# Hybrid decoder block on one core: order and halves of the first loads and casts, a warm-up on another operand, and other buffers for the down projection's weight chunks

## The chip, the cores and the metric

The kernel runs on one core of a Trainium2 chip. The metric is device time of one execution in microseconds (us); lower is better. Where several runs were made, the median is given. Engines are named as the profile names them: PE does matrix products (PEld is its loading of weights), DVE is the vector engine, ACT the scalar engine, POOL is GpSimd, SP only issues transfers. A name with a q behind it (SPq, ACTq, POOLq) is an engine's instruction stream issuing a DMA.

## The reference, cut to what matters

The input is x of 512 rows and 1024 columns in float32. All weights are float32.

```python
h = rmsnorm(x, pre_mix_norm)
q_r, k_r, v_r, g_r, q_s, k_s, v_s, gate_r, gate_s = split(h @ w_in)
y_r = (silu(g_r) * groupnorm(retention(q_r, k_r, v_r))) @ w_ret_out
y_s = sliding_window_attention(q_s, k_s, v_s, sinks) @ w_swa_out
x = x + rmsnorm((sigmoid(gate_r) * y_r + sigmoid(gate_s) * y_s) @ w_out, post_mix_norm)
h = rmsnorm(x, pre_mlp_norm)
u = square(relu(h @ w_up))
x = x + rmsnorm(u @ w_down, post_mlp_norm)
```

The change touches the very first product (k_s and v_s, together 256 columns of w_in) and the last one (u @ w_down, where w_down has 4096 rows and 1024 columns).

## The kernel before, in words

**Two-part operands.** A float32 factor is cut into a high part and a low part: `split` (L156) lets ACT cast the source to the rounded type fp32r (the high part, L158), and DVE subtract that from the source (the low part, L160). `split_scaled` (L400) does the same for a source times the pre-norm gain gT (ACT L402, DVE L403). `mm3` (L215) makes each product from three matmuls: high by high (L218), high by low (L219), low by high (L220). Its second argument is the moving operand: for k_s and v_s that is the weights `wkv`, and `xg` is loaded as the stationary one. So the first L218 needs the high parts of xg and wkv, the first L219 needs the low part of wkv, the first L220 the low part of xg.

**The start.** x comes transposed in eight blocks of 128 x 512, `xTs[:, k]`, and the weights of k_s and v_s in eight pieces of 128 x 256, `raw_kv[:, k]`. SP issues them in turn; the piece for k = 0 is issued by ACT, behind the gain. Until the first operands are there, ten products of the identity with itself (WARM, L397) keep PE at work. Then the loop at L409 does two splits and twelve matmuls for each k, into four PSUM banks `ptok`. Two query blocks (tile `pblk`, split from `raw_q`) follow, then the matmuls that spread the row factors (L451), two more query blocks, and from then on blocks that read the normalized input `hT`, which DVE and ACT make from `xTs` in `norm_input` (L427). Next come the `wide` products of v_r, and between them the window attention: scores into `swa_s` (L506), a softmax on DVE (L520 to L538) and ACT (L527), and transposes of the probabilities `s` on PE (L550, L552), first for one head of a pair and then for the other.

**The end.** The up projection runs in sixteen pairs, `up_pair` (L1274). The three that matter here are the last steps of the last pair: `last["chain"]`, `last["chain2"]` and `last["chain3"]` are the ACT copies of its sums. The down projection is a Strassen-Winograd scheme over 2 x 2 blocks: the steps at L1373 (`step_p1`, `step_p2`, `step_p5` for four chunks j each), then `step_p6`, `step_p3`, `step_p7` (L1421 to L1446) and p4. A step splits a chunk of u (`left`, L1313, 128 x 1024 at a time) and a chunk of w_down (`right`, L1318, two halves of 128 x 1024), and then makes 24 matmuls of 128 x 512 (`product2`). The chunks of w_down, 1 MB each, come in two kinds. `tch[j]` stays for several steps and has other chunks added to it by transfers that POOL issues (`t_add`, L1333). `load_b` (L1336) brings chunks that are used once or twice.

**Buffers and order.** `raw_tile` (L162) hands out two buffers in turn, which the whole kernel shares; a transfer into one waits until the split of its last content is done. `dpool3` (L1301) uses space that the up projection frees, so a transfer into it waits for the last products that read from there. Each engine does its instructions in the order in which they are queued. That order is made before the run, from priorities (`tc.high_priority`) and from explicit edges: `tc.issue_after(ins)` queues what a block contains behind `ins` on that engine.

Of the kernel before, what the change touches and what calls it, by code (L numbers as in the profile page):

```python
# [10 lines left out]
F32 = mybir.dt.float32  # L11
# [5 lines left out]
P = 128  # L17
D_MODEL = 1024
# [13 lines left out]
CHAIN_AHEAD = 400  # L32
SUMS_AHEAD = 0
HSUM_AHEAD = 400
WARM = 10
LEFT_AHEAD = 300
T2_DMA = 4
ENTRY = 32
# [2 lines left out]
C_QR, C_KR, C_VR, C_GR, C_QS, C_KS, C_GATE_R = (0, 512, 1024, 2048, 3072, 3584, 3840)  # L41
# [63 lines left out]
def f(ap):  # L105
    return ap.bitcast(F32)
# [3 lines left out]
def block_kernel(ctx, tc, x, xT, pre_mix, w_in, w_qk, w_v, w_g, w_gate, w_ret, w_swa, w_out, sinks, post_mix,  # L110
                 pre_mlp, w_up, w_down, post_mlp, decay, chunk, dist, out):
    nc = tc.nc
    x, out = x[0], out[0]
    w_in, w_ret, w_swa, w_out = (w[0] for w in (w_in, w_ret, w_swa, w_out))
# [6 lines left out]
    def bank(shape, name="ps"):  # L121
        return psum.tile(shape, F32, tag="ps", name=name)
# [5 lines left out]
    ident = const.tile([P, P], F32, name="ident")  # L128
# [25 lines left out]
    last = {}  # L154

    def split(hi, lo, src):  # L156

        last["hi"] = nc.scalar.copy(hi, src)  # L158
        last["prior"] = last.get("split")
        last["split"] = nc.vector.tensor_tensor(lo, src, f(hi), op=ALU.subtract)  # L160

    def raw_tile(shape):  # L162
        return stream.tile(shape, F32, name="raw", tag="raw", bufs=2)

    def place(shape, front=False):

        whole = stream.tile([P, 1024 + 64], F32R, name="whi", tag="whi")
        flat = whole[:, :1024] if front else whole[:, 16 : 16 + 1024]
        dims = " ".join("abc"[: len(shape) - 1])
        sizes = {n: shape[i + 1] for i, n in enumerate("abc"[: len(shape) - 1])}  # L170
        hi = flat.rearrange(f"p ({dims}) -> p {dims}", **sizes)
        if "wlo" not in last:
            pad(stream, 64)
            last["wlo"] = True
        return hi, stream.tile(shape, F32R, name="wlo", tag="wlo")

    def parts(src, shape, front=False):
        hi, lo = place(shape, front)
        split(hi, lo, src)
        return hi, lo  # L180
# [34 lines left out]
    def mm3(ps, a, b, first, last, more=False):  # L215

        (ah, al), (bh, bl) = a, b
        nc.tensor.matmul(ps, ah, bh, start=first, stop=False, skip_group_check=more)  # L218
        nc.tensor.matmul(ps, ah, bl, start=False, stop=False, skip_group_check=more)  # L219
        return nc.tensor.matmul(ps, al, bh, start=False, stop=last, skip_group_check=more)  # L220
# [147 lines left out]
    xTs = xTpool.tile([P, KD, SEQ], F32, name="xTs", tag="xs")  # L368
    xgctx = ExitStack()
    xgpool = xgctx.enter_context(tc.tile_pool(name="xgpool", bufs=1, side="right"))  # L370
    gT = xgpool.tile([P, KD], F32, name="gT")
    xg = [xgpool.tile([P, KD, SEQ], F32R, name=f"xg{i}") for i in range(2)]
    xctx = ExitStack()
    xpool = xctx.enter_context(tc.tile_pool(name="xpool", bufs=1))
    ones = xpool.tile([P, P], F32, name="ones")
    wkv = [xpool.tile([P, KD, 256], F32R, name=f"wkv{i}") for i in range(2)]

    nc.vector.memset(ones, 1.0)
    raw_kv = raw_tile([P, KD, 256])
    for k in range(KD):  # L380
        nc.sync.dma_start(xTs[:, k], xT[k])
        if k == 0:
            nc.scalar.dma_start(gT, pre_mix)
        queue = nc.scalar if k == 0 else nc.sync
        queue.dma_start(raw_kv[:, k], w_in[k * P : (k + 1) * P, C_KS : C_KS + 256])
    raw_q = raw_tile([P, KD, 256])
    for i in range(2):
        rows = slice(i * D_MODEL // 2, (i + 1) * D_MODEL // 2)
# [6 lines left out]
        nc.sync.dma_start(xts[t], x[t * P : (t + 1) * P, :])  # L395
    warm = bank([P, P], "warm")
    for _ in range(WARM):  # L397
        nc.tensor.matmul(warm, ident, ident, start=True, stop=True)

    def split_scaled(hi, lo, src, scale):  # L400

        nc.scalar.mul(hi, src, scale)  # L402
        nc.vector.scalar_tensor_tensor(lo, src, scale, f(hi), op0=ALU.mult, op1=ALU.subtract)  # L403

    def xcol(k, t):
        return tuple(a[:, k, t * P : (t + 1) * P] for a in xg)

    kv_ps = [bank([P, 256], "ptok") for _ in range(NT)]
    for k in range(KD):  # L409
        split(wkv[0][:, k], wkv[1][:, k], raw_kv[:, k])  # L410
        split_scaled(xg[0][:, k], xg[1][:, k], xTs[:, k], gT[:, k : k + 1])
        for t in range(NT):
            mm3(kv_ps[t], xcol(k, t), tuple(a[:, k] for a in wkv), k == 0, k == KD - 1)

# [675 lines left out]
    for bp in range(KD // 2):  # L1090
# [3 lines left out]
        for b in range(2):  # L1094
            hi = mpool.tile([P, SEQ], F32R, name="mhi", tag="m")
# [30 lines left out]
    for half in range(2):  # L1126
# [11 lines left out]
        with tc.high_priority(offset=CHAIN_AHEAD):  # L1138
            for t in range(2):
# [4 lines left out]
                for n in range(2):  # L1144
                    c = slice(n * 512, (n + 1) * 512)
# [110 lines left out]
    dpool2 = ctx.enter_context(tc.tile_pool(name="dpool2", bufs=1, side="right"))  # L1256
    uc[2] = dpool2.tile([P, 4, 4, 256], F32, name="uc2")
    tch = [None] * 4

    def load_t(j):  # L1260
        pool = dpool2 if j == 0 else dpool3
        tch[j] = pool.tile([P, 4, 512], F32, name=f"tch{j}")
        nc.sync.dma_start(tch[j], w_down[0, 0, j])

    usum = []
# [8 lines left out]
    def up_pair(fp, a):  # L1274
# [19 lines left out]
        return a  # L1294

    load_t(0)
    a = wino_first(up_weights(NH))
    for fp in range(NH, 16):
        a = up_pair(fp, a)
    uctx.close()  # L1300
    dpool3 = ctx.enter_context(tc.tile_pool(name="dpool3", bufs=1))  # L1301
    for j in range(1, 4):
        load_t(j)
    g_out = dpool3.tile([P, D_MODEL], F32, name="g_out")
    nc.sync.dma_start(g_out, post_mlp.to_broadcast([P, D_MODEL]))
    p1c = [dpool3.tile([P, 512], F32, name="p1c", bufs=2) for _ in range(2)]
    p15 = [dpool3.tile([P, 512], F32, name="p15", bufs=2) for _ in range(2)]
    u3 = [dpool3.tile([P, 512], F32, name="u3", bufs=2) for _ in range(2)]
# [4 lines left out]
    def left(j, q):  # L1313
        hi, lo = (ring.tile([P, 4, 256], F32R, name=f"left{i}") for i in range(2))
        split(hi, lo, uc[j][:, q])
        return hi, lo

    def right(src):  # L1318
        return [parts(src[:, 2 * i : 2 * i + 2], [P, 2, 512]) for i in range(2)]
# [8 lines left out]
    def product2(ps, j, a, b):  # L1328
        for h in range(2):
            for tb in range(2):  # L1330
                product(ps, a, b, h, j == 0, j == 3, tb)

    def t_add(dst, k, c, j):  # L1333
        nc.gpsimd.dma_start(dst, w_down[k, c, j], accum_op=ALU.add)

    def load_b(k, c, j, alone=2):  # L1336
        raw = stream2.tile([P, 4, 512], F32, name="rb") if j == alone else raw_tile([P, 4, 512])
        nc.sync.dma_start(raw, w_down[k, c, j])
        return raw

    stream2 = ctx.enter_context(tc.tile_pool(name="stream2", bufs=1))
# [7 lines left out]

    def step_p1(j):  # L1350
        with tc.high_priority(offset=LEFT_AHEAD if j == 0 else 0):
            with tc.issue_after(last["chain"].ins):
                a = left(j, 0)
            with tc.issue_after(last["chain2"].ins):
                b = right(tch[j])
        t_add(tch[j], 0, 1, j)
        product2(p1, j, a, b)

    def step_p2(j):
        with tc.issue_after(last["chain2"].ins), tc.high_priority(offset=LEFT_AHEAD if j == 0 else 0):  # L1360
            a, b = left(j, 2), right(load_b(1, 0, j, 4))
        product2(p2, j, a, b)
# [10 lines left out]
    for step, j in ((step_p1, 0), (step_p2, 0), (step_p1, 1), (step_p5, 0), (step_p2, 1),  # L1373
                    (step_p1, 2), (step_p5, 1), (step_p2, 2), (step_p1, 3), (step_p5, 2),
                    (step_p2, 3), (step_p5, 3)):
        step(j)

    outz = [None] * NT
    ms0 = [None] * NT
# [39 lines left out]
    rb = {}  # L1419
# [18 lines left out]
    for j in range(4):  # L1438
        rb[j] = load_b(1, 1, j)
        step_p6(j)  # L1440
        step_p3(j)
        if j == 0:
            p7 = banks2("p7")
        else:
            step_p7(j - 1)
# [16 lines left out]
    for j in range(2):  # L1462
        a, b = left(j, 3), right(tch[j])
# [21 lines left out]
    for i in range(2):  # L1485
        c = slice(i * 256, (i + 1) * 256)
# [54 lines left out]
```

## Time and profile before

| | us |
|---|---|
| median of 3 runs | 715.14 |
| the three runs | 715.14, 717.18, 713.86 |
| the profiled execution | 716.0 |
| span of its instructions | 714.2 |

The span is counted from the first profiled instruction to the last, and 1.8 us of the profiled execution's own time lie around it. All positions below are microseconds from the span's start. In a row of the timeline the first number is the start, the second the duration, and a bracket at the end gives how long the engine was idle before it and what ended the idle time. "x20" is a count. In a table of windows each engine has its busy time and, in brackets, its count of instructions; DMA share is the mean busy share of the 16 DMA engines.

| engine | busy us | share of the span |
|---|---|---|
| PE | 705.6 | 99% |
| PEld | 631.6 | 88% |
| DVE | 535.0 | 75% |
| ACT | 431.4 | 60% |
| POOL | 63.0 | 9% |

### The profile page before, as it was taken

To read this page: it belongs to the slowest core of one execution; us is meant where nothing else is said; L and a number is where in the kernel's file an instruction comes from. 1 tells how busy PE (TensorE), PEld (TensorE's weight loads), DVE (VectorE), ACT (ScalarE), POOL (GpSimd) and SP (SyncE) were. 2 spreads that over 40 slices of the span, in tenths; PEclk is the share of its full clock that TensorE was granted. 3 is DMA by queue.
4 is the path that set the end of the run, shared out by engine and by line. 5 is a ranking of instruction groups with operands and counts; after the bars stand their busy time and mean duration, and the time that the engine had idled before them with its cause. 6 is when DMAs were issued, how large, how long until landed. Compare 5 with 4: busy or idle time off the path is not lost.

```text
span 714.2 us, 11458 instructions
## 1 busy us (share of the span) xinstructions
PE 705.6 (99%) x4528; PEld 631.6 (88%) x4528; DVE 535.0 (75%) x800; ACT 431.4 (60%) x733; POOL 63.0 (9%) x78
## 2 busy tenths in 40 slices
PE   9999999999999999999999999999999999999996
PEld 8887789898888999989888999999999888888885
DVE  6598978685975667566945876777777787977797
ACT  6657876566655625435733866766668656555571
POOL 0210000121100000000011100000000000010010
PEclk9999999999999999999999999999999999999998
DMA  9964723866444455553662619776753999698603
GB/s 319 331 173 84 163 60 125 244 155 140 90 145 121 126 141 149 155 169 98 217 257 78 162 45 284 199 195 174 197 150 119 329 270 237 145 208 195 117 1 117
DMA packets 40613, 119.37 MB, mean 167 GB/s; under 512 B 3568, under 2 KB 17008, under 8 KB 34416
## 3 DMA queue, kind: packets, MB, share of 16 engines
q1 hardware_dynamic: 33504, 81.28, 32.6%
q0 software_dynamic: 6768, 37.23, 28.0%
q8 instruction: 35, 0.57, 0.3%
q10 hardware_dynamic: 288, 0.14, 0.1%
q14 instruction: 18, 0.15, 0.1%
HBM read 116.54 MB, written 2.10 MB: 166 GB/s over the span
## 4 chain that ended last, share of the span: by engine, by line
PE 91%; DVE 4%; DMA 2%; issue 1%; ACT 1%; POOL 0%; POOLq 0%; DVEq 0%; SPq 0%; ACTq 0%
PE wino L218 9%; PE wino L219 9%; PE wino L220 9%; PE p L220 5%; PE p L219 5%; PE p L218 5%; PE wide L218 4%; PE wide L219 4%; PE wide L220 4%; PE pblk L220 2%; PE pblk L219 2%; PE pblk L218 2%; PE yr L220 2%; PE yr L218 2%; PE ps L218 2%; PE ps L220 2%
## 5 line engine op out<-in xcount | busy, mean ns | idle before, releaser
L160 DVE TENSOR_TENSOR wlo<-raw,whi 128x1024 fp32r<-128x1024 f32 (+1 forms) x80 | 96.3, 1208 | 43.7 <-ACT whi L158 43.6
L158 ACT CAST whi<-raw 128x1024 fp32r<-128x1024 f32 (+1 forms) x80 | 82.8, 1041 | 31.4 <-DMA raw<-in_w_down 7.7
L220 PE MATMUL p<-whi,left 128*128 128x512 f32 x216 | 84.1, 390 | 0.2 <-DVE left L160 0.2
L219 PE MATMUL p<-wlo,left 128*128 128x512 f32 x216 | 84.2, 390 | 0.0
L218 PE MATMUL p<-whi,left 128*128 128x512 f32 x216 | 84.0, 390 | 0.1
L220 PEld LDWEIGHTS p<-whi,left 128*128 128x128 f32 x216 | 40.5, 188 | 9.4 <-DVE left L160 1.1
L219 PEld LDWEIGHTS p<-wlo,left 128*128 128x128 f32 x216 | 40.5, 188 | 8.8 <-DVE wlo L160 0.3
L218 PEld LDWEIGHTS p<-whi,left 128*128 128x128 f32 x216 | 40.5, 188 | 8.7 <-ACT left L158 0.5
L158 ACT CAST p<-rs 128x1024 fp32r<-128x1024 f32 x22 | 23.1, 1052 | 36.5 <-DVE rs L272 36.4
L160 DVE TENSOR_TENSOR wlo<-tch,whi 128x1024 fp32r<-128x1024 f32 x32 | 38.6, 1219 | 7.5 <-ACT whi L158 7.5
L158 ACT CAST left<-uc 128x1024 fp32r<-128x1024 f32 x28 | 29.3, 1051 | 22.8 <-PE p L219 20.9
L160 DVE TENSOR_TENSOR left<-uc,left 128x1024 fp32r<-128x1024 f32 x28 | 34.1, 1220 | 9.9 <-ACT left L158 9.9
L158 ACT CAST whi<-tch 128x1024 fp32r<-128x1024 f32 x32 | 33.2, 1050 | 11.8 <-PE p L220 6.5
L160 DVE TENSOR_TENSOR p<-rs,p 128x1024 fp32r<-128x1024 f32 x22 | 27.0, 1225 | 16.7 <-ACT p L158 16.7
L160 DVE TENSOR_TENSOR wlo<-rs,whi 128x1024 fp32r<-128x1024 f32 x23 | 28.1, 1223 | 12.9 <-ACT whi L158 10.3
L218 PE MATMUL wino<-h2s,p 128*128 128x256 f32 x104 | 28.7, 276 | 0.0
L219 PE MATMUL wino<-h2s,p 128*128 128x256 f32 x104 | 28.7, 276 | 0.0
L220 PE MATMUL wino<-h2s,p 128*128 128x256 f32 x104 | 28.7, 276 | 0.0
L218 PE MATMUL wino<-h2c,whi 128*128 128x256 f32 x104 | 28.7, 276 | 0.0
L219 PE MATMUL wino<-h2c,whi 128*128 128x256 f32 x104 | 28.7, 276 | 0.0
L220 PE MATMUL wino<-h2c,wlo 128*128 128x256 f32 x104 | 28.7, 276 | 0.0
L218 PE MATMUL wino<-h2s,whi 128*128 128x256 f32 x104 | 28.7, 276 | 0.0
(410 smaller groups left out, 2352.1 us busy)
## 6 DMA issues: line engine op xcount, KB each, us to landing
tch<-in_w_down POOLq DMA_DIRECT2D x12, 1024.0 KB, 9.9
raw<-in_w_down SPq DMA_DIRECT2D x7, 1024.0 KB, 7.6
rs<-in_w_up SPq DMA_DIRECT2D x13, 512.0 KB, 4.5
rs<-in_w_up POOLq DMA_DIRECT2D x13, 512.0 KB, 5.5
raw<-in_w_up SPq DMA_DIRECT2D x13, 512.0 KB, 5.3
acc<-in_w_v POOLq DMA_DIRECT2D x4, 1024.0 KB, 8.0
rs<-in_w_gate SPq DMA_DIRECT2D x8, 512.0 KB, 3.8
acc<-in_w_g POOLq DMA_DIRECT2D x4, 1024.0 KB, 8.0
```

The lines of the kernel that those rows point to most:

```text
L158: last["hi"] = nc.scalar.copy(hi, src)
L160: last["split"] = nc.vector.tensor_tensor(lo, src, f(hi), op=ALU.subtract)
L218: nc.tensor.matmul(ps, ah, bh, start=first, stop=False, skip_group_check=more)
L219: nc.tensor.matmul(ps, ah, bl, start=False, stop=False, skip_group_check=more)
L220: return nc.tensor.matmul(ps, al, bh, start=False, stop=last, skip_group_check=more)
```

## The change

Four edits at the start. The first piece of the weights is issued by SP between the first and the second block of x, and no longer by ACT. The block of x for k = 0 is split in two halves of 256 columns, with the split of the weights queued in between. The tile `ones` is set first on DVE, and the warm-up multiplies it with itself, seven times in place of ten.

In the down projection the chunks `tch[1]` and `tch[2]` move into the two shared raw buffers, and are loaded from behind `step_p2(0)`; `tch[3]` stays in `dpool3` and is loaded, with the last gain, behind `step_p2(1)`. In exchange `load_b` takes the raw buffer only for its first chunk, and a ring of two in `dpool3` for the others. In `step_p1(0)` the right operand's first half is split ahead of the left operand, and its second half behind it.

```diff
-WARM = 10
+WARM = 7
...
-    nc.vector.memset(ones, 1.0)
+    with tc.high_priority(offset=1000):
+        nc.vector.memset(ones, 1.0)
...
-        queue = nc.scalar if k == 0 else nc.sync
-        queue.dma_start(raw_kv[:, k], w_in[k * P : (k + 1) * P, C_KS : C_KS + 256])
+        nc.sync.dma_start(raw_kv[:, k], w_in[k * P : (k + 1) * P, C_KS : C_KS + 256])
...
-        nc.tensor.matmul(warm, ident, ident, start=True, stop=True)
+        nc.tensor.matmul(warm, ones, ones, start=True, stop=True)
...
-        split(wkv[0][:, k], wkv[1][:, k], raw_kv[:, k])
-        split_scaled(xg[0][:, k], xg[1][:, k], xTs[:, k], gT[:, k : k + 1])
+        halves = (slice(0, 256), slice(256, 512)) if k == 0 else (slice(0, 512),)
+        for i, c in enumerate(halves):
+            split_scaled(xg[0][:, k, c], xg[1][:, k, c], xTs[:, k, c], gT[:, k : k + 1])
+            if i == 0:
+                split(wkv[0][:, k], wkv[1][:, k], raw_kv[:, k])
...
     def load_t(j):
-        pool = dpool2 if j == 0 else dpool3
-        tch[j] = pool.tile([P, 4, 512], F32, name=f"tch{j}")
+        if j in (1, 2):
+            tch[j] = raw_tile([P, 4, 512])
+        else:
+            tch[j] = (dpool2 if j == 0 else dpool3).tile([P, 4, 512], F32, name=f"tch{j}")
         nc.sync.dma_start(tch[j], w_down[0, 0, j])
...
-    for j in range(1, 4):
-        load_t(j)
     g_out = dpool3.tile([P, D_MODEL], F32, name="g_out")
-    nc.sync.dma_start(g_out, post_mlp.to_broadcast([P, D_MODEL]))
...
     def load_b(k, c, j, alone=2):
-        raw = stream2.tile([P, 4, 512], F32, name="rb") if j == alone else raw_tile([P, 4, 512])
+        if (k, c, j) == (1, 0, 0):
+            raw = raw_tile([P, 4, 512])
+        elif j == alone:
+            raw = stream2.tile([P, 4, 512], F32, name="rb")
+        else:
+            raw = dpool3.tile([P, 4, 512], F32, name="rd", bufs=2)
...
     def step_p1(j):
         with tc.high_priority(offset=LEFT_AHEAD if j == 0 else 0):
+            with tc.issue_after(last["chain2"].ins):
+                b = [parts(tch[j][:, :2], [P, 2, 512])] if j == 0 else right(tch[j])
             with tc.issue_after(last["chain"].ins):
                 a = left(j, 0)
-            with tc.issue_after(last["chain2"].ins):
-                b = right(tch[j])
+            if j == 0:
+                with tc.issue_after(last["hi"].ins), tc.issue_after(last["split"].ins):
+                    b.append(parts(tch[j][:, 2:], [P, 2, 512]))
...
         step(j)
+        if (step, j) == (step_p2, 0):
+            load_t(1)
+            load_t(2)
+        elif (step, j) == (step_p2, 1):
+            load_t(3)
+            nc.sync.dma_start(g_out, post_mlp.to_broadcast([P, D_MODEL]))
```

## The prediction, made before the changed kernel was run

> **What bounds the kernel now.** I began with the page's busy times, and then asked who makes PE wait.
>
> ```profile
> span 714.2 us, 11458 instructions
> PE 705.6 (99%) x4528; PEld 631.6 (88%) x4528; DVE 535.0 (75%) x800; ACT 431.4 (60%) x733; POOL 63.0 (9%) x78
> ```
>
> ```profile
> PE warm L398 <- POOL ident masks.py:199: 1.3, 1, 1.3
> PE ptok L218 <- ACT wkv L158: 0.3, 1, 0.3
> PE p L220 <- DVE left L160: 0.2, 1, 0.2
> ```
>
> PE is without work for 8.6 us of 714.2, and waits only three times, for 1.8 us together; most of the rest is the tail behind its last product. So no edit in the middle can pay much. What can be won is time in which PE is busy and useless: the warm-up, and products at a low clock. The timeline shows the start:
>
> ```profile
> 0.73 0.86 SPq L381 DMA_DIRECT2D xTs<-in_xT  x2
> 1.23 0.39 ACTq L385 DMA_DIRECT2D raw<-in_w_in  x1
> 1.35 4.64 PE L398 MATMUL warm<-ident 128*128 128x128 f32 x20 [1.35 <-POOL ident masks.py:199]
> 1.63 0.17 DVE L378 MEMSET ones<- 128x128 f32 x1
> 3.61 0.72 ACT L402 ACTIVATE xg<-xTs,gT 128x512 fp32r<-128x512 f32 x1 [0.95 <-DMA gT<-in_pre_mix_norm]
> 4.88 0.72 ACT L402 ACTIVATE xg<-xTs,gT 128x512 fp32r<-128x512 f32 x1 [0.55 <-DMA xTs<-in_xT]
> 5.51 0.69 ACT L158 CAST wkv<-raw 128x256 fp32r<-128x256 f32 x2
> 6.26 0.58 PE L218 MATMUL ptok<-wkv,xg 128*128 128x256 f32 x1 [0.27 <-ACT wkv L158]
> 6.78 0.58 PE L219 MATMUL ptok<-wkv,xg 128*128 128x256 f32 x1
> 10.78 0.29 PE L219 MATMUL ptok<-wkv,xg 128*128 128x256 f32 x1
> ...
> 7.16:10.57 3.41, 3.41 (x18) 3.41 (x17) 3.41 (x7) 3.13 (x7) 0.00 (x0) 1.00 1.03 351
> 10.57:19.55 8.98, 8.98 (x80) 8.98 (x80) 5.70 (x12) 6.33 (x11) 0.55 (x1) 1.00 1.02 379
> ```
>
> The last two rows are windows. ACT casts the weights only behind the second block of x, for which it idles 0.55 us, so the second product starts at 6.78. In the first window 16 of the 18 products begin, one every 0.213 us; in the second 79, one every 0.114 us. The clock doubles at about 10.8 (a product drops from 0.58 to 0.29 us), 9.4 us after the warm-up began and 4.0 us after the stream became unbroken at 6.78. With 95 products from the second on, and the clock up at time r, the stage ends at 10.80 + 0.533 * start + 0.467 * r; for 6.78 and 10.8 that is 19.46, and the trace has 19.55.
>
> **The start, step by step.** Today the weights' transfer (ACT's row at 1.23) took 3.8 us, beside the second block of x:
>
> ```profile
> raw<-in_w_in ACTq DMA_DIRECT2D x1, 128.0 KB, 3.8
> ...
> xTs<-in_xT SPq DMA_DIRECT2D x1, 256.0 KB, 2.6
> ```
>
> The second row is the first block of x, landed at 0.73 + 2.6 = 3.4. Moved to SP behind that block, the weights land between 3.4 and today's 5.0; with 128 KB at the 351 GB/s of the first window, 0.37 us behind it, I take 3.8. ACT still begins at 3.6, held by the gain. Half a scaled block lies between half of 0.72 and 0.72; I take 0.42. A 128 x 256 cast takes 0.39 (two in 0.69, overlapped, in the row at 5.51). So ACT has the first half of xg at 4.03 and the weights' high part at 4.42, the first product starts near 4.47, and the low part (DVE, two instructions of about 0.42 behind 4.03, as in the row at 13.15 below) lets the second start at 4.95 in place of 6.78. Every later SP issue goes back one place, about 0.43 us. I cost that at nothing, since landings follow the busy DMA engines and not the issue; without that cover it costs 0.43. ACT loses a 0.39 us issue in a time when it waits anyway, and one extra instruction on ACT and on DVE (0.1 us each) falls into the 0.55 us for which ACT waits.
>
> `ones` is ready at about 0.8 + 0.17, so the warm-up starts near 1.03; seven tenths of 4.64 us end it at 4.28, and PE has next to no gap up to 4.47. When does the clock rise? The earliest is 4.0 us after 1.03, so 5.0, if the warm-up counts; the latest is 4.0 us after 4.95, so 8.95, if the small gaps (0.19 us, then 0.27 us ahead of 4.95) undo it. That it was undone before, with gaps of 0.27 us and another pause ahead of 6.78, speaks for the middle, and I take 7.5. The stage then ends at 10.80 + 2.64 + 3.50 = 16.9; the bounds give 15.8 and 17.6.
>
> One floor lies under that. The operands come at their own rate:
>
> ```profile
> 13.15 0.42 DVE L160 TENSOR_TENSOR wkv<-raw,wkv 128x256 fp32r<-128x256 f32 x1
> ```
>
> In both windows the DMA share is over 1, and the last weights have their low part at 13.57 (the row at 13.15). A k takes 12 * 0.114 = 1.36 us at the high clock, and the second k is ready at about 6.7, so seven of them end no earlier than 6.7 + 9.6 = 16.3. PE is thus ahead of before by 1.9 to 3.3 us at the end of this stage, 2.6 as I take it.
>
> The Trainium skill, page "TensorE: Matmul & The Clock Gate", section "Part 1: The HAM clock gate", says that the clock doubles after one whole busy window of about 3.4 us, and that the windows run freely. By that, as an estimate from the page, the clock rises between 4.4 and 7.9, but if a gap spoils a window between 8.3 and 11.8. The same page of the Trainium skill, section "Why this matters for your kernels", advises at least 4 us of matmuls as a warm-up, which speaks against seven products (3.25 us by the row at 1.35). The trace agrees with a window that was spoilt, and cannot show which of the two it will be.
>
> **Where the lead is cut.** PE gets ahead; what it meets is work tied to transfers. I followed ACT, DVE and PE forward:
>
> ```profile
> raw<-in_w_in SPq DMA_DIRECT2D x1, 512.0 KB, 14.1
> ...
> 33.09 1.05 ACT L158 CAST whi<-raw 128x1024 fp32r<-128x1024 f32 x1
> 34.05 1.13 ACT L158 CAST hT<-xTs 128x512 fp32r<-128x512 f32 x2
> 34.69 1.29 DVE L160 TENSOR_TENSOR hT<-xTs,hT 128x512 fp32r<-128x512 f32 x2 [0.99 <-ACT hT L158]
> ...
> 25.00:33.00 8.00, 8.00 (x41) 6.75 (x40) 5.80 (x7) 3.81 (x5) 2.46 (x5) 1.00 1.10 317
> ...
> 34.69:58.97 24.28, 24.28 (x120) 19.58 (x119) 24.25 (x29) 12.78 (x18) 3.93 (x3) 1.00 0.58 154
> 59.00:66.20 7.20, 7.20 (x33) 5.83 (x32) 6.86 (x30) 7.19 (x23) 0.01 (x1) 1.00 0.79 148
> ...
> 65.09 1.08 DVE L538 TENSOR_SCALAR s<-s,den 128x128 f32<-128x128 f32 x4
> ...
> 68.06 0.60 PE L550 MATMUL psd<-ident,s 128*128 128x128 f32 x4
> ```
>
> The transfer in the first row is issued at 18.95 and lands 14.1 us later, at 33.0, behind a queue that keeps the DMA engines full (share 1.10). ACT casts it at 33.09; only behind that in its queue come the casts of hT at 34.05, and DVE, which waits for them, starts at 34.69 and then has no idle time up to 58.97. From there the softmax keeps ACT busy (7.19 of 7.20 us) to the end of the second head's scaling at 66.17. PE transposes that head at 68.06. None of this moves when PE is early: with 0.06 us for the signal, PE's slack there is 68.06 - 66.23 = 1.83 us, or 2.16 if only the last of the four transposes waits (three places of 0.11 later). So of a lead of 2.6 us some 0.6 comes back as a new wait at about 66.2, and I take a gain of **2.0 us** (1.8 to 2.2).
>
> **The down projection.** Here the first steps show a stall:
>
> ```profile
> 546.13 0.33 SPq L1338 DMA_DIRECT2D raw<-in_w_down  x1
> ...
> 548.27 2.00 ACT L158 CAST whi<-tch 128x1024 fp32r<-128x1024 f32 x2
> 549.36 2.36 DVE L160 TENSOR_TENSOR wlo<-tch,whi 128x1024 fp32r<-128x1024 f32 x2 [2.22 <-ACT whi L158]
> 551.64 2.35 DVE L160 TENSOR_TENSOR left<-uc,left 128x1024 fp32r<-128x1024 f32 x2
> 552.35 0.40 PE L218 MATMUL p<-whi,left 128*128 128x512 f32 x1
> 552.91 0.50 PE L220 MATMUL p<-whi,left 128*128 128x512 f32 x1 [0.16 <-DVE left L160]
> 553.24 0.40 PE L218 MATMUL p<-whi,left 128*128 128x512 f32 x1
> 553.91 2.35 DVE L160 TENSOR_TENSOR wlo<-raw,whi 128x1024 fp32r<-128x1024 f32 x2
> ...
> 556.22 1.55 SPq L1263 DMA_DIRECT2D tch<-in_w_down x3
> 562.58 2.95 ACT L158 CAST whi<-tch 128x1024 fp32r<-128x1024 f32 x3 [2.25 <-DMA tch<-in_w_down]
> 567.77 1.05 ACT L158 CAST whi<-raw 128x1024 fp32r<-128x1024 f32 x1 [0.35 <-PE p L220]
> ```
>
> A product of 128 x 512 follows the last after 0.23 us; here 0.56 and 0.33 us pass, so 0.43 us are lost, while DVE does both halves of the chunk ahead of the left operand. With one half moved behind it, the left low part is ready at 551.7 and not at 552.9, ahead of its use: the stall goes, **0.43 us**. The moved half is ready by 552.9, and PE needs it twelve products behind 551.9, at 554.6. What is late next is the DMA wait at 562.58, which is ACT's and not among PE's three; `tch[1]` now goes into the raw buffer that the transfer at 546.13 takes today, so it goes too, and I count it as nothing. The waits that are added: `tch[2]` waits on SP for the split of the first `load_b` chunk, which ends at 556.26 (the row at 553.91). Behind it queue the chunk of `step_p2(1)`, issued at 546.13 today, then `tch[3]` and the gain. As the second of three chunks issued from 556.2 on, of which the first was there at 562.58, the chunk of `step_p2(1)` lands some 3.0 us later (1 MB at the 351 GB/s of the first window), near 565.6; ACT casts it only at 567.77, so 2.2 us cover it.
>
> **Sum.** 716.0 (the profiled execution) - 2.0 - 0.43 = 713.5. This execution is 0.9 us above the median of 715.14; the three runs differ by 3.3 us, in part perhaps by when their clock rose. With the lead cut at the softmax the new time hangs less on that, so I do not take the 0.9 off again. It is 0.2% under the median. About 0.5%, 3.6 us, is what a measurement of this kernel tells from no change.
>
> **The rivals.** (a) *The queues of ACT and DVE come out in another order near 31 to 34 us*, so that hT does not stand behind the transfer, and nothing cuts the lead: 2.6 to 3.3 us and the 0.43, so 712.3 to 713.0. For it: the order is made anew for the new start. Against: that transfer's place depends on buffers that the change does not touch there.
> (b) *The clock rises as late as before*, 9.4 us behind the warm-up's start: at 10.4. The stage ends at 18.3, a lead of 1.2 us, below the cut: 716.0 - 1.2 - 0.43 = 714.4. For it: a shorter warm-up and two small gaps. In the Trainium skill's page on the clock gate this case is the spoilt window.
> (c) *Slower: the new order puts more work on DVE ahead of the softmax.* DVE has no idle time from 34.69 to 58.97, so each instruction of 1.2 us that is queued ahead shifts the second head's scaling by 1.2. One eats 1.2 of the slack of 1.83; from 2.3 us on (1.83 + 0.43) the kernel is slower than before. Three give 66.17 + 3.6 = 69.8, PE 1.8 us late, 717.4; two give 716.2. For it: DVE is that full. Against: no edit adds work there.
> (d) *The change does not bring the products forward*, since ACT still casts the weights behind the second block of x. Then only the 0.43 us and perhaps some of the clock are won: about 715.3.
>
> **Chances.** Forecast 0.5, (a) 0.2, (b) 0.15, (c) 0.08, (d) 0.07. The range takes in the forecast's 713.3 to 713.8, (a), (b) and (d), and half a microsecond for the scatter: 711.7 to 716.2. It leaves out most of (c). Faster by over 0.5% means under 711.56; only the far end of (a) with the scatter gets there: 0.07. Slower by over 0.5% means over 718.7: four or more instructions in (c), 0.03. Within 0.5%: 0.90.
>
> **What would show it.** Right: the second product near 4.95, products every 0.11 us by about 7.5, the first pblk product near 17, a new wait of PE for DVE at the transposes near 66, none at 552. Wrong: the cast of wkv behind the second xg; the clock up after 9; no wait at 66 (then rival a); new waits of PE for a down-projection chunk; or a stage between 70 and 545 in which PE's lead changes.

## The result, and the profile after

The changed kernel takes 719.47 us (median of 6 runs, 718.96 to 719.94), the kernel before 714.61 (median of 6). The ratio is 1.0064, with an interval of 1.0047 to 1.008. The change made the kernel slower by 0.6%, and the time lies outside the prediction's range of 711.7 to 716.2. The profiled execution took 719.31 with a span of 717.5, 3.3 more than the profiled execution before. One execution of the run old_warm below (1105.3 us, at a granted clock of 0.599) is left out of that run's ratio.

The list of PE's waits in the kernel after comes first, with its total, its count and the longest:

```profile
PE pblk L219 <- DVE hT L160: 1.4, 1, 1.4
PE warm L398 <- DVE mhalf L131: 1.0, 1, 1.0
PE ptok L218 <- ACT wkv L158: 1.0, 2, 0.6
PE R L454 <- DVE diag L428: 0.6, 1, 0.6
PE pblk L220 <- DVE wlo L160: 0.5, 1, 0.5
PE pblk L218 <- ACT whi L158: 0.4, 1, 0.4
PE pblk L218 <- ACT hT L158: 0.2, 1, 0.2
```

Before, there were three waits. The one at the down projection (`p L220 <- DVE left`) is gone. Six are new or longer, and four of those stand at `pblk`, in products that read `hT`, where before there was none. The forecast had looked for a new wait at 66 us; there is none. PE's timeline at the start:

```profile
1.04 3.35 PE L398 MATMUL warm<-ones 128*128 128x128 f32 x14 [1.04 <-DVE mhalf L131]
5.02 0.74 PE L218 MATMUL ptok<-wkv,xg 128*128 128x256 f32 x4 [0.62 <-ACT wkv L158]
5.59 0.37 PE L219 MATMUL ptok<-wkv,xg 128*128 128x256 f32 x1
...
17.15 0.39 PE L218 MATMUL pblk<-xg,whi 128*128 128x512 f32 x1
```

The start does what was forecast: the first product is at 5.02 (before 6.26), and the two query blocks begin at 17.15 (before 19.55, forecast 16.9), a lead of 2.40 us. The loss comes later. These are windows of the kernel after, from the last product of the query blocks that read `xg` to the first scores:

```profile
41.56:49.07 7.51, 4.97 (x19) 2.93 (x17) 6.44 (x9) 6.05 (x8) 0.00 (x0) 1.00 0.69 248
49.07:52.48 3.41, 3.41 (x8) 2.71 (x9) 3.41 (x5) 0.10 (x1) 0.00 (x0) 0.50 0.45 167
52.48:58.17 5.69, 5.69 (x26) 4.33 (x24) 5.37 (x6) 3.03 (x5) 0.91 (x1) 1.00 0.66 114
```

And the same stretch of the kernel before, in one window:

```profile
42.93:54.34 11.41, 11.41 (x51) 9.02 (x49) 11.38 (x13) 6.98 (x10) 0.91 (x1) 1.00 0.69 177
```

The columns are the stretch, then busy time and count of PE, PEld, DVE, ACT and POOL, the granted clock of PE, DMA share and GB/s. The same products took 11.41 us before and 16.61 after: 5.20 us lost. Of those, some 3.6 go in the first row, in which PE waits or restarts (busy 4.97 of 7.51), and in the second row the clock is at 0.50 for 3.41 us, in which a product takes 0.427 us and not 0.227; eight of them cost 1.6. The chain of waits of the kernel after leads back to where this starts (start, duration, what):

```profile
29.10 14.26 DMA raw<-in_w_in
43.35 0.02 issue
43.38 1.06 ACT whi L158
44.43 0.02 issue
44.46 1.23 DVE wlo L160
45.68 1.33 DVE xTs L431 x2
47.01 0.66 DVE qs L493
47.67 0.66 DVE xTs L431
48.33 0.61 DVE hT L160
48.94 0.04 issue
48.99 0.75 PE pblk L219
```

The transfer is the weights of the first blocks on `hT` (L194). It was issued at 29.10. Here is SP's timeline in the kernel after,

```profile
14.77 3.36 SPq L697 DMA_DIRECT2D acc<-in_w_v  x1
27.30 0.33 SPq L478 DMA_DIRECT2D dist_sb<-in_dist  x1
27.68 0.42 SPq L480 DMA_DIRECT2D sink_sb<-in_sinks  x1
28.16 0.42 SPq L699 DMA_DIRECT2D acc<-in_w_v  x1
28.62 1.06 SPq L194 DMA_DIRECT2D raw<-in_w_in  x2
```

and in the kernel before:

```profile
14.02 2.76 SPq L694 DMA_DIRECT2D acc<-in_w_v  x1
16.82 0.83 SPq L696 DMA_DIRECT2D acc<-in_w_v  x1
18.53 7.99 SPq L194 DMA_DIRECT2D raw<-in_w_in  x2
28.85 0.76 SPq L475 DMA_DIRECT2D dist_sb<-in_dist  x1
29.65 0.49 SPq L477 DMA_DIRECT2D sink_sb<-in_sinks  x1
```

Read the order, not only the times. Before, the two loads of weights (L194) stand ahead of the loads of the small tables `dist_sb` and `sink_sb`. After, the tables stand ahead, and two transfers of weights (the second half of `acc`, and L194) behind them. The tables live in space that is free only when the row factors' products (tile R) have been made; those end at 27.24, and the load of `dist_sb` is issued at 27.30. SP does its queue in order. The buffer of the L194 weights was free from 19.54 on, when DVE's split of its last content ends (before at 18.51, and they were issued at 18.53). So these weights stood for 9 us behind a small table that had no room yet. Nobody edited those lines: the order is made anew from priorities, and it came out another way.

The down projection of the kernel after begins without its stall:

```profile
555.71 0.39 PE L218 MATMUL p<-whi,left 128*128 128x512 f32 x1
555.94 0.40 PE L219 MATMUL p<-wlo,left 128*128 128x512 f32 x1
556.17 0.39 PE L220 MATMUL p<-whi,left 128*128 128x512 f32 x1
556.40 0.39 PE L218 MATMUL p<-whi,left 128*128 128x512 f32 x1
```

From the first of these products to PE's last it takes 155.16 us, before 155.66. The whole account, as PE's place against the kernel before: -2.40 at 17.15, +1.03 up to 41.56 (most of it the new wait at R), +5.20 up to 58.17, -0.50 in the down projection: +3.33. The spans differ by 3.3. The medians differ by 4.9, since the profiled execution before was 1.4 us over its median.

### The profile page after: what moved, and what is told of

Read it like the earlier page. It is cut to its first block, busy times and chain, and to the rows that moved or that the text cites. A ratio compares the mean times of both kernels' runs of the same rounds, so it can differ in the third digit from the quotient of the medians.

```text
span 717.5 us, 11450 instructions
## 1 busy us (share of the span) xinstructions
PE 705.6 (98%) x4522; PEld 629.6 (88%) x4522; DVE 535.5 (75%) x801; ACT 431.9 (60%) x734; POOL 61.1 (9%) x78
## 4 chain that ended last, share of the span: by engine, by line
PE 86%; DMA 5%; DVE 5%; issue 2%; ACT 1%; SPq 1%; POOL 0%; POOLq 0%; DVEq 0%; ACTq 0%
PE wino L218 9%; PE wino L220 9%; PE wino L219 9%; PE p L218 5%; PE p L219 5%; PE p L220 5%; PE wide L218 4%; PE wide L219 4%; PE wide L220 4%; DMA raw<-in_w_in 3%; PE yr L218 2%; PE ps L218 2%; PE ps L220 2%; PE yr L219 2%; PE yr L220 2%; PE ps L219 2%
## 5 line engine op out<-in xcount | busy, mean ns | idle before, releaser
L160 DVE TENSOR_TENSOR wlo<-raw,whi 128x1024 fp32r<-128x1024 f32 (+1 forms) x78 | 94.0, 1208 | 42.1 <-ACT whi L158 42.1
L158 ACT CAST whi<-raw 128x1024 fp32r<-128x1024 f32 (+1 forms) x78 | 80.6, 1039 | 23.9 <-DMA raw<-in_w_in 7.2
L218 PE MATMUL p<-whi,left 128*128 128x512 f32 x216 | 84.0, 390 | 0.1
L219 PE MATMUL p<-wlo,left 128*128 128x512 f32 x216 | 84.0, 389 | 0.0
L220 PE MATMUL p<-whi,left 128*128 128x512 f32 x216 | 84.0, 390 | 0.0
L220 PEld LDWEIGHTS p<-whi,left 128*128 128x128 f32 x216 | 40.5, 188 | 8.8 <-DVE left L160 0.4
L218 PEld LDWEIGHTS p<-whi,left 128*128 128x128 f32 x216 | 40.5, 188 | 8.8 <-ACT left L158 0.5
L219 PEld LDWEIGHTS p<-wlo,left 128*128 128x128 f32 x216 | 40.5, 188 | 8.5
L160 DVE TENSOR_TENSOR wlo<-rs,whi 128x1024 fp32r<-128x1024 f32 x23 | 28.1, 1223 | 13.0 <-ACT whi L158 10.3
L158 ACT CAST whi<-rd 128x1024 fp32r<-128x1024 f32 x18 | 18.9, 1051 | 17.8 <-DMA rd<-in_w_down 9.1
L218 PE MATMUL wino<-h2s,p 128*128 128x256 f32 x104 | 28.8, 277 | 0.0
L220 PE MATMUL wino<-h2s,p 128*128 128x256 f32 x104 | 28.7, 276 | 0.0
L219 PE MATMUL wino<-h2s,p 128*128 128x256 f32 x104 | 28.7, 276 | 0.0
L218 PE MATMUL wino<-h2c,whi 128*128 128x256 f32 x104 | 28.7, 276 | 0.0
L219 PE MATMUL wino<-h2c,whi 128*128 128x256 f32 x104 | 28.7, 276 | 0.0
L220 PE MATMUL wino<-h2c,wlo 128*128 128x256 f32 x104 | 28.7, 276 | 0.0
L218 PE MATMUL wino<-h2s,whi 128*128 128x256 f32 x104 | 28.7, 276 | 0.0
L219 PE MATMUL wino<-h2s,whi 128*128 128x256 f32 x104 | 28.7, 276 | 0.0
## 6 DMA issues: line engine op xcount, KB each, us to landing
rd<-in_w_down SPq DMA_DIRECT2D x6, 1024.0 KB, 10.5
```

## The experiments

Three theories at first. **Q**: the loss is the order of SP's queue. **S**: the loss is the first weights' move to SP's queue, which makes the whole stream of transfers late; in the trace after, the second block of x lands at 6.04 (before 4.86) and the two halves of the query weights at 15.23 and 16.68 (before 14.16 and 15.64). **D**: the loss is in the down projection's buffers. Two more came up on the way: **C**, the moment at which the clock rises, and **K**, the copies of `kv` on ACT.

| run | weights L194 issued | first pblk | to the last pblk on xg | from there to swa_s | median | ratio, interval |
|---|---|---|---|---|---|---|
| before | 18.53 | 19.55 | 23.38 | 11.41 | 714.3 to 714.6 | |
| after | 28.62 | 17.15 | 24.41 | 16.61 | 719.47 | 1.0064 (1.0047, 1.008) |
| down_only | 18.51 | 17.80 | 23.39 | 11.41 | 714.07 | 0.9989 (0.9972, 1.0006) |
| start_only | 29.17 | 18.56 | 23.57 | 15.97 | 719.41 | 1.0064 (1.0044, 1.0084) |
| before_head | 28.98 | 18.11 | 23.39 | 15.62 | 718.73 | 1.0056 (1.0038, 1.0074) |
| late_dist | 18.59 | 16.70 | 23.65 | 11.41 | 714.06 | 0.9989 (0.9972, 1.0007) |
| ones10 | 28.32 | 17.34 | 23.76 | 14.96 | 720.05 | 1.0073 (1.0058, 1.0088) |
| old_warm | 19.32 | 17.82 | 23.39 | 11.41 | 714.46 | 1.0001 (0.9992, 1.001) |
| late_dist_w10 | 19.17 | 16.80 | 24.17 | 11.41 | 713.89 | 0.9989 (0.9979, 1.0) |
| late_dist_act_w10 | 19.41 | 16.93 | 24.59 | 11.40 | 713.73 | 0.9987 (0.9978, 0.9996) |
| late_dist_w10_kv | 19.49 | 17.50 | 23.56 | 11.41 | 713.18 | 0.998 (0.9971, 0.9989) |
| late_dist_act_w10_kv | 18.72 | 17.18 | 23.37 | 11.41 | 713.12 | 0.9979 (0.9969, 0.9988) |

All in us; the ratio is that to the kernel before, run beside each. The places and stretches are those of SP's issues and of PE's products in each run's one trace. The fifth column sorts the runs by itself: 11.41 wherever the weights are issued near 19, 15.0 to 16.6 wherever they stand behind the tables.

**down_only** is the kernel before with the down projection's edits alone (the last five hunks of the diff).

> The kernel before with the down projection's edits alone. Theory Q (the loss is at the start of the kernel: on SP the transfer of the weights for the first hT block now stands behind the two small loads for the attention, lands at 41 to 43 us and not at 31 to 33, and PE waits): this kernel has none of that and gains the stall of 0.43 us at 552, so 714.2 against 714.6. Theory D (the down projection's buffers cost the time): 719 or more. Theory S (the first weights on SP's queue make all early transfers 1.0 to 1.5 us late, and this alone costs the time): 714.2, as Q.

Measured 714.07. D falls. The list of PE's waits of this run has one row left:

```profile
PE warm L398 <- POOL ident masks.py:199: 1.4, 1, 1.4
```

From the down projection's first product to PE's last it takes 155.32 us, 0.34 less than before. The median alone does not show that gain: the interval of the ratio takes in 1.

**start_only** is the other half: the kernel before with the four edits at the start.

> The kernel before with the four edits at the start alone, the down projection as before. Theories Q and S: the whole loss and 0.4 us more, 719.9. Theory D: under 714.6.

Measured 719.41. The whole loss is in the start's edits.

**before_head** makes only the suspected order, in the kernel before. Nothing of the change is in it.

```diff
-    nc.sync.dma_start(sink_sb, sinks.to_broadcast([P, SWA_HEADS]))
+    last["sink"] = nc.sync.dma_start(sink_sb, sinks.to_broadcast([P, SWA_HEADS]))
...
-        nc.sync.dma_start(sy, w_[0, 0])
+        with ExitStack() as queue:
+            if w_ is w_v:
+                queue.enter_context(tc.issue_after(last["sink"].ins))
+            nc.sync.dma_start(sy, w_[0, 0])
...
-    wqk = load_qk(0)
+    with tc.issue_after(last["sink"].ins):
+        wqk = load_qk(0)
```

> The kernel before with one thing changed: on SP the second load of w_v's sums and the weights of the first hT block are queued behind the two small attention loads, as they stand in the changed kernel. No edit of the change is in it. Theory Q: those small loads wait for the row factors' products at about 28 us, so the weights land near 41 to 43, PE waits for them and for hT between 43 and 50, and the time is 717 to 720. Theories S and D: no change, 714.6. If the wait is there but PE's clock stays up, the lower end; if the clock drops for one stretch of 3.4 us as in the changed kernel, 1.7 us more.

Measured 718.73, 4.4 us over the kernel before beside it, where the change costs 4.9: the order alone is enough for nearly all of the loss. S and D had expected nothing here.

**late_dist** takes the order out of the changed kernel, by writing the two loads behind the weights.

```diff
-    nc.sync.dma_start(dist_sb, dist)
-    nc.sync.dma_start(sink_sb, sinks.to_broadcast([P, SWA_HEADS]))
-    nc.gpsimd.tensor_scalar(nsink_sb, sink_sb, -1.0, None, op0=ALU.mult)
...
     wqk = load_qk(0)
+    nc.sync.dma_start(dist_sb, dist)
+    nc.sync.dma_start(sink_sb, sinks.to_broadcast([P, SWA_HEADS]))
+    nc.gpsimd.tensor_scalar(nsink_sb, sink_sb, -1.0, None, op0=ALU.mult)
```

> The changed kernel with the two small attention loads (and the negation of the sinks on POOL) written behind the load of the first hT block's weights, so that SP has them in the order of the kernel before. Theory Q: the waits of PE between 41 and 50 us go, the weights land at 32 to 35, and the start's lead of about 1.4 us and the down projection's 0.4 remain: 712.8 (712.2 to 713.5). Theory S: still 718 to 719. Theory D: still 719.

Measured 714.06. The loss is gone, and SP's timeline of this run has the old order,

```profile
18.59 7.38 SPq L194 DMA_DIRECT2D raw<-in_w_in  x2
26.16 3.21 SPq L791 DMA_DIRECT2D dist_sb<-in_dist  x1
```

but the gain that I expected beside it (712.8) is not there: with all four edits of the start and a good order the kernel is where down_only is without them. The trace of this run is of its fastest execution (712.90), so it does not show where the others lose the lead. That was the next question.

**ones10** asks first which of the four edits turns the order round. It is the kernel before with the warm-up's operand and the place of one memset changed.

```diff
-    nc.vector.memset(ones, 1.0)
+    with tc.high_priority(offset=1000):
+        nc.vector.memset(ones, 1.0)
...
-        nc.tensor.matmul(warm, ident, ident, start=True, stop=True)
+        nc.tensor.matmul(warm, ones, ones, start=True, stop=True)
```

> The kernel before with one thing changed: ten warm-up products on ones instead of the identity, and the memset of ones first. No transfer moves by hand, no halves, the down projection as before. Theory Q (the loss is the order of SP's queue, which this edit alone turns round: the loads of dist and the sinks, which wait for room that R's products free, come out ahead of the weights of the first hT block): 718.0 to 719.5, with those weights issued behind 27 us. Theory S (the loss comes from the transfer moved to SP at the start): no loss, 713.9 to 714.6. Theory D (down projection): no loss.

Measured 720.05, half a microsecond over what Q expected. Its SP timeline has the tables at 27.00 and the weights behind them:

```profile
27.00 0.33 SPq L476 DMA_DIRECT2D dist_sb<-in_dist  x1
27.38 0.42 SPq L478 DMA_DIRECT2D sink_sb<-in_sinks  x1
27.86 0.42 SPq L697 DMA_DIRECT2D acc<-in_w_v  x1
28.32 1.06 SPq L194 DMA_DIRECT2D raw<-in_w_in  x2
```

The operand of products whose result nobody reads, with the memset that serves it, costs 5.8 us, and the loss arises some 25 us later and on another engine's queue. What the half microsecond over comes from is not shown. The trace is of the fastest of the four executions (718.42, within Q's range), and it already holds a wait that the other runs do not have (`p L219` for DVE, 0.8 us in the list).

**old_warm** is the opposite: the changed kernel with the old warm-up (ten products on the identity, the memset in its old place), everything else of the change kept.

> The changed kernel with the old warm-up alone put back (ten products on the identity, the memset of ones in its old place); the first weights stay on SP, the halves and the down projection stay changed. Theory Q: the weights of the first hT block are issued at 18 to 19 us again and the loss is gone, 713.3 to 714.4. Theory S: the moved transfer still delays the stream, so a good part of the loss stays, 716 to 719.

Measured 714.46, 0.06 over Q's range. No loss, with the first weights still on SP's queue: S falls as the cause of the loss. But no gain either: the first pblk product is at 17.82, and in down_only, which has none of the start's edits, at 17.80. That the order turns on the warm-up (its operand and the memset that serves it) is thereby shown from both sides. Which of the two turns it, and by which rule of the planning, stays open.

**late_dist_w10** is late_dist with ten warm-up products, for theory C.

> The run late_dist (loads of dist and the sinks behind the weights) with ten warm-up products in place of seven. Theory C (late_dist's median hangs on when the clock rises: its warm-up of 3.36 us and the pause of 0.7 us behind it let it rise at 4.5 or only near 10.5, from execution to execution): the warm-up now runs to 5.3 and no pause follows, the clock rises by 7.9 in every execution, the first pblk product starts between 16.5 and 17.4, median 712.7 to 713.6, and the executions lie within 1.2 us. Rival (the lead is taken back later, by operands or by the softmax): 714.0 to 714.3 as in late_dist, spread as there (712.9 to 714.7).

Measured 713.89, between 712.51 and 715.78. The stage ends at 16.80 in the trace, within C's bounds, but the median and the spread are the rival's: C alone does not explain where the lead goes.

**late_dist_act_w10** is late_dist_w10 with the first weights on ACT's queue again.

```diff
-        nc.sync.dma_start(raw_kv[:, k], w_in[k * P : (k + 1) * P, C_KS : C_KS + 256])
+        queue = nc.scalar if k == 0 else nc.sync
+        queue.dma_start(raw_kv[:, k], w_in[k * P : (k + 1) * P, C_KS : C_KS + 256])
```

> The run late_dist_w10 with the first weights back on ACT's queue. Theory S in its weak form (one queue alone starts the stream more slowly, and the operands are the floor of the first stage): the second block of x lands at 4.4 to 4.9 in place of 5.5 to 6.0 and everything behind it 0.6 to 1.0 us earlier, the first products start some 0.4 us later, and the time is 0.3 to 0.9 us under late_dist_w10. If the operands are not the floor: as late_dist_w10 or up to 0.3 us over it.

Measured 713.73, 0.16 us from late_dist_w10. The second block of x lands at 4.43 (there 4.89, 5.59 in late_dist), but no gain shows: the weak form of S is not borne out either. The trace showed something else. Its timeline around R:

```profile
24.16 0.48 ACT L474 ACTIVATE kv<-ptok,rstd 128x256 f32<-128x256 f32 x1 [0.49 <-POOL rstd L151]
24.53 1.05 ACT L426 ACTIVATE junk<-xt 128x1024 f32<-128x1024 f32 x1
...
26.86 0.49 PE L455 MATMUL R<-diag,ones 128*128 128x128 f32 x2 [0.93 <-DVE diag L429]
```

ACT squares the fourth tile of x (`junk`) only at 24.53, behind three copies of `kv`, although that tile landed at 22.43. In the kernel before, the last of the four squares stands ahead of the four copies:

```profile
21.77 1.06 ACT L422 ACTIVATE junk<-xt 128x1024 f32<-128x1024 f32 x1 [0.15 <-DMA xt<-in_x]
22.83 1.55 ACT L470 ACTIVATE kv<-ptok,rstd 128x256 f32<-128x256 f32 x4
```

PE needs the factor that comes of it at R, and waits 0.93 us. So the new order has a second effect, on ACT: it can take the start's lead back at R. The fourth column of the table shows the price: 23.38 to 23.39 in the kernel before, down_only, before_head and old_warm, where ACT has the old order, and 24.17 to 24.59 in late_dist_w10, the kernel after and this run. In the traces of start_only, late_dist and ones10 ACT has the new order too, but PE comes to R late enough, or the tiles early enough, and the price is 0.2 to 0.4 us.

**late_dist_w10_kv** and **late_dist_act_w10_kv** put ACT's old order back in the last two.

```diff
-        nc.scalar.activation(junk, xts[t], AF.Square, accum_out=ss[:, 0:1])
+        last["square"] = nc.scalar.activation(junk, xts[t], AF.Square, accum_out=ss[:, 0:1])
...
-        nc.scalar.mul(kv[:, t, :], kv_ps[t], rstd[t])
+        with tc.issue_after(last["square"].ins):
+            nc.scalar.mul(kv[:, t, :], kv_ps[t], rstd[t])
```

> The run late_dist_w10 with ACT's four copies of kv put behind its four squares of the x tiles, as they stand in the kernel before. Theory K (the start's lead is taken back at R: behind the new order ACT squares the fourth x tile only after three copies of kv, its diag ends at 26.07, and PE waits there, 0.3 us by the list of waits and 0.5 by its pitch): the fourth diag ends at 23.5 to 24.2, the wait at R is gone, the first swa_s product starts 0.4 to 0.6 us earlier for the same first pblk product, median 713.2 to 713.6. Rival (the scatter of the clock alone hides the lead): no change, 713.8 to 714.0.

> The run late_dist_act_w10 with the same edit. There the wait at R was 0.9 us by the list and 1.1 by PE's pitch, so theory K expects the first swa_s product some 1.0 us earlier for the same first pblk product (near 35.0 us behind it in place of 36.0) and a median of 712.6 to 713.2, under both kernels. Rival: no change, 713.6 to 713.9.

Measured 713.18 and 713.12, the first 0.02 under K's range and the second within it, and both faster than the kernel before beyond the interval, by 0.2%. The wait at R is gone in both lists of waits, and the fourth column is back at 23.56 and 23.37. One detail missed: in late_dist_w10_kv the fourth diag ended at 25.43 and not by 24.2, since the tiles of x landed 1.35 us later in that execution. Against the runs without the edit (713.89 and 713.73) the step is 0.6 to 0.7 us; their intervals overlap, so its size is less sure than its place. Taken together, 12 of the 22 executions without the edit took over 713.7 us, and one of the 22 with it. late_dist itself, with seven warm-up products, was not run with this edit. The two queues for the first weights give 713.18 and 713.12: no difference.

## Why the prediction was wrong

**The step that failed** is the one about SP: "Every later SP issue goes back one place, about 0.43 us. I cost that at nothing, since landings follow the busy DMA engines and not the issue". Both halves fail. In the first stage the issues went back by about a place, and the landings with them by about 1 us (the second block of x at 6.04, before 4.86). Behind it the queue came out in another order, and there too the landing followed the issue. The transfer on which the forecast rested ("issued at 18.95") was issued at 29.10, 10.2 us later, and cast at 43.38, before at 33.09: 10.3 later. PE needs these weights near 42 to 43, so this used up all their slack. "None of this moves when PE is early" held for an early PE, but not for another order; against rival (a) it said that "that transfer's place depends on buffers that the change does not touch there". The trace before shows what its place depends on beside buffers: what stands ahead of it in SP's queue.

**The rivals.** Rival (a) had the right mechanism, a re-made order, but only as a gain. What it named did come. In late_dist ACT casts three blocks of `hT` at 32.35, ahead of the weights at 34.21 and 36.11, where before they stood behind the weights (34.05 behind 33.09), and the second head's scaling ends at 65.31 and not at 66.17. Rival (c), the slower case, looked for more work on DVE ahead of the softmax, and for four instructions or more before it would show. What came was a transfer that starts late and then holds ACT, DVE and PE one behind the other. Neither rival asked what could change places in SP's queue.

**The start.** For this execution the place was nearly right: the first blocks at 17.15 (16.9), the first product at 5.02 (4.47). Part of that is luck. The clock was up by 4.7 and not at 7.5, earlier than the prediction's earliest (5.0). By its own pace of 0.114 us, 95 products from 5.2 on would then end near 16.0, as an estimate. Operands that came late took about 1.1 back: PE waits for a cast of `wkv` again at 7.13, and restarts slowly. The order "second product near 4.95" was off, as four L218 came first and the first L219 followed at 5.59. But the term of 2.0 us was sized against one execution, and that one had a late clock (10.8, where the three others below have 7.4 to 7.6). The three other traces with the old warm-up (down_only, old_warm, before_head) reach the first pblk product at 17.80, 17.82 and 18.11, not at 19.55, so the lead of 17.15 over those is 0.65 to 0.96 us. The line that let this pass is "I do not take the 0.9 off again". The lead also comes with the warm-up more than with the transfer and the halves that the prediction followed step by step: ones10, with the new operand and its memset alone, has its first pblk product at 17.34, and old_warm, with the moved transfer and the halves but the old warm-up, at 17.82 (one trace each). And where the lead was cut, that was at R, at 26, and not at the softmax: late_dist has no wait at 66, where PE's transposes of the second head start at 65.48, 0.17 us behind its scaling. With R's cut removed the start and the down projection together are worth 1.3 to 1.4 us against the median of 714.5 beside them, where the forecast lay 1.6 under its median.

**The clock** did not rise at one place for one start. By the first clock record of each trace it rose at 7.4 to 7.6 in three of the four traces with the warm-up on the identity, which starts at 1.35, and at 10.8 in the fourth. With the warm-up on `ones`, which starts at 1.04, it rose at 4.1 to 5.1 in seven of eight, and at 10.5 in the eighth (start_only). Where it rises that early, the end of ten warm-up products runs faster, as in late_dist_act_w10 (3.92 us, on the identity 4.64):

```profile
1.04 3.92 PE L399 MATMUL warm<-ones 128*128 128x128 f32 x20 [1.04 <-DVE mhalf L131]
```

Whether the operand, the 0.3 us or chance makes this difference no run separates. Here are windows of start_only, and then one of down_only:

```profile
5.02:10.50 5.48, 5.48 (x26) 5.48 (x27) 4.46 (x10) 4.77 (x10) 0.00 (x0) 1.00 1.01 355
10.50:18.56 8.06, 8.06 (x73) 8.06 (x72) 5.20 (x10) 5.15 (x10) 0.00 (x0) 1.00 1.01 369
```

```profile
7.60:17.80 10.20, 10.20 (x92) 10.20 (x91) 7.29 (x14) 7.34 (x14) 0.00 (x0) 1.00 1.05 380
```

In start_only a product takes 0.21 us up to 10.5, and 0.11 from there; in down_only it takes 0.11 from 7.6 on. The clock column says 1.00 throughout, since a trace has no clock record ahead of the first rise; there the pace of the products tells the clock. The kernel after has the same start as start_only, and its products come every 0.11 us from 5.8 on. The Trainium skill, page "TensorE: Matmul & The Clock Gate", section "Part 1: The HAM clock gate", says that the window is free-running, so that the same kernel shows another count of slow products from run to run. The traces agree: at 4.7 and at 10.5 for one start. How much of the spread between executions is this stays open, since there is one trace of each kernel.

**The down projection** was right: 0.43 forecast, 0.34 measured alone and 0.50 in the whole change, by PE's places in one trace each. Its new waits on SP cost nothing, as argued: PE has no wait there in either trace.

## What to carry to other kernels

Where the order of the queues is planned anew for every version, an edit can cost most where it edits nothing: compare the order of every queue before and after, transfers first, and ask of each transfer that waits for space what stands behind it. Keep a load that waits for another stage's buffers behind the loads that do not, by an explicit edge and not by luck. And before sizing a gain against one profiled execution, set its time against the median: what that execution lost by chance is no gain that the change can bring.

## What the runs showed of the hardware

**Half a clock for a broken stretch.** In the kernel after, PE was idle for no longer than 1.43 us at a time between 41.56 and 49.07, and busy for 4.97 of these 7.51 us, and yet the granted clock fell to 0.50 for 3.41 us behind it. The run before_head shows the same spell of 3.41 us from 45.0 on, behind waits of 1.57 and 0.53 us. In start_only and ones10, with waits of up to 1.72 and 0.77 us, it did not fall. So the waits cost more than their length in some executions.

**One queue starts the stream more slowly.** With the first weights on SP's queue, the bytes per second dip between 4.0 and 5.25 us. These are the DMA view's rows of the kernel after and of the kernel before, a column for each quarter of a microsecond from 0:

```profile
GB/s 0 0 0 0 0 0 16 165 57 207 366 351 329 328 320 295 238 143 279 225 209 352 324 373 369 369 340 377 402 381 397 397 389 410 361 324 209 164 246 311
```

```profile
GB/s 0 0 0 0 0 0 0 180 82 190 358 357 386 389 348 340 365 316 311 361 332 361 340 365 352 352 365 361 377 357 393 414 377 340 287 336 352 348 348 348
```

From the seventeenth column on, five have 238, 143, 279, 225 and 209 after, and 365, 316, 311, 361 and 332 before. The lowest of these five columns is 53 to 143 in the six traces with one queue, and 291 to 348 in the six with two. The Trainium skill, page "DMA: Bandwidth & Descriptors", section "Issuing engines are not separate DMA queues", says that issuing from several engines only saves the sequencer's issue time. Here the blocks behind the dip landed up to 1.2 us later, more than the one issue of 0.43 us; the time of the kernel did not show it (713.18 and 713.12).
